# Reciprocal softmax sums stored in rows, gates and attention outputs laid out by token block, queries and keys asked for ahead

## The chip, the cores and the metric

The kernel runs on one NeuronCore of a Trainium2 chip. The metric is the device time of one execution in microseconds; beside the timed runs there is one profiled execution, whose trace is read here.

## What is computed

Two layers of a decoder trunk over 2048 tokens of width 1024, all in float32. Layer 0 runs two groups of eight heads side by side behind one input projection: latent attention (MLA, query and key of width 96) and forgetting attention (FoX, width 64, with a cumulative log forget gate added to the scores). Both are causal. Layer 1 is sliding-window attention with 16 query heads and 2 key heads. In each layer the attention output is multiplied by a SiLU gate, projected, added to the scaled input and normalized:

```
p = softmax(sc)                                   # causal, per head
o = concat([_merge(o_mla), _merge(o_fox)])        # 2048 x 1024
y = (o * silu(gate)) @ w_out
x = layer_norm(ALPHA * x + y)
```

The change touches layer 0 only: its softmax sums, its gate, its attention output and its query and key loads.

## The kernel before

Every matrix product is split: an operand is the sum of a high and a low part, and a product takes two or three matmuls. The program has five phases.

**Phase 1** (`phase1`) projects layer 0's input in chunks of 512 tokens. `feature_tile` applies the SiLU to a tile of 128 gate features by 512 tokens and stores it to the DRAM tensor `g1`, laid out [feature, token] (lines 349 to 352).

**Phase 2** (`phase2`) is layer 0's attention. It walks over 16 heads (even `n`: MLA, odd `n`: FoX) and, in each, over four chunks `c` of 512 queries. The generator `produce(n, c)` makes the scores and exponentials of four query blocks of 128; `consume(n, c)`, one chunk later, transposes the exponentials and multiplies them by the values (P V). The two are interleaved by hand: at each turn the one that is less far along goes on, by the weights of `weights`. `produce` loads the chunk's queries into `q0` (MLA: also `q1`), of which there are two buffers each; `load_head` loads a head's keys (`ka`, `kb`), values (`vv`) and, for FoX, the forget sums (`cb`), two buffers each, and is called at a head's first chunk (line 515). The softmax isn't normalized here. Each query block's sum of exponentials goes to a column of `su`; after four blocks `produce` takes reciprocals and stores them to the DRAM tensor `rd`, [head, token]. The tile holds one query per partition, so neighbouring tokens lie in different partitions and the store is made of single four-byte elements:

```
nc.vector.reciprocal(out=rec[:], in_=su[:])
nc.sync.dma_start(out=rd[h if mla else 8 + h, tcs].rearrange("(j p) -> p j", p=128), in_=rec[:])
```

`finish` in `consume` stores a chunk's output for one head to `og1[c]`, [128, 8, 512] (line 591).

**Phase 3** (`phase3`) is layer 0's output projection, block by block of 128 tokens. `load_og(t)` loads the block's gates into `oh`, the reciprocals into `ol` (each head's row of 128 tokens is read by 64 partitions), and the attention output into `og`, which has one buffer; POOL multiplies `og` by the gate, VectorE by the reciprocals, ScalarE and VectorE split it into high and low (lines 794 to 802). `out_block` makes 48 matmuls per block, adds the residual and collects the statistics; the normalization of two blocks is done together, in part on POOL (lines 759 to 773). The first two blocks are prepared at the end of phase 2 by `prefetch`, in one load of 256 tokens: POOL multiplies gate by reciprocals, then each block by that product (lines 649 to 654).

**Phases 4 and 5** are layer 1. Its reciprocal sums (`factors`) are transposed on TensorE and stored as 16 rows of 128 (lines 1074 to 1078).

Nearly all transfers are issued from SyncE's queue (SP). The order of each engine's instructions is set before the run by the framework: it goes by the order in which they are written, but moves one ahead when, by its own estimate, its inputs and its buffer are there earlier. On each queue they then run strictly in that order, each waiting for its semaphores. `keep_in_program_order` pins an instruction behind the one written before it on its engine.

Of the kernel before, what the change touches and what calls it, by code (L numbers as in the profile page):

```python
# [17 lines left out]
T = 2048  # L18
# [21 lines left out]
def decoder_trunk(ctx, tc, x, x_t, w_lat, w_main, w_u, g_lat, b_f, w_out1, ln1,  # L40
# [17 lines left out]
    kf = [dram.tile([8, 64, T], F32, name=f"kf{i}") for i in range(2)]  # L58
    vd = [dram.tile([2, 128, NB, 512], F32, name=f"vd{i}") for i in range(2)]
    cd = dram.tile([8, T], F32, name="cd")  # L60
    rd = dram.tile([16, T], F32, name="rd")
    g1 = dram.tile([D, T], F32, name="g1")
    og1 = [dram.tile([128, KB, 512], F32, name=f"og1_{c}") for c in range(4)]
    x1 = dram.tile([T, D], F32, name="x1")
    qs = [[dram.tile([16, 32, T], F32, name=f"qs{i}{s}") for s in range(2)] for i in range(2)]
    ks = [[dram.tile([2, 32, T], F32, name=f"ks{i}{s}") for s in range(2)] for i in range(2)]
# [119 lines left out]
    def phase1(late):  # L186
# [145 lines left out]
        def feature_tile(n, m, chunk, xT, w):  # L332

            (xh, xl), (wh, wl) = xT, w
            ms = tok(m)
            tcs = slice(chunk * 512, (chunk + 1) * 512)
            ps = ps_m.tile([128, 512], F32, name="pm")
            mm3(ps[:], [(wh[:, k, ms], wl[:, k, ms], xh[:, k, :], xl[:, k, :]) for k in range(KB)])
            if n < 4:
                dst = qf if n < 2 else kf  # L340
                p = (n % 2) * 2 + m
                hi = stg.tile([128, 512], F32R, name="s_hi")
                lo = stg.tile([128, 512], F32R, name="s_lo")
                split_ps(hi[:], lo[:], ps[:])
                for i, t in enumerate((hi, lo)):
                    nc.sync.dma_start(out=dst[i][2 * p:2 * p + 2, :, tcs].rearrange("h d t -> (h d) t"), in_=bits(t[:]))
            else:
                p = (n - 6) * 2 + m
                sg = stg.tile([128, 512], F32, name="s_x", bufs=3)
                nc.scalar.activation(out=sg[:], in_=ps[:], func=AF.Silu)  # L350
                queue = nc.gpsimd if (p, chunk) == (7, 3) else nc.sync
                queue.dma_start(out=g1[p * 128:(p + 1) * 128, tcs], in_=sg[:])

        k_heads = None
        sums = forget_sums(pool, fl, ps_t, ps_m)
# [118 lines left out]
            nc.sync.dma_start(out=cb[:], in_=cd[h:h + 1, :].broadcast_to([128, T]))  # L474
        return ka, kb_, vv, cb

    def load_gate(gt, rb, t0, n):

        nc.sync.dma_start(out=gt, in_=g1[:, t0:t0 + n].rearrange("(k p) t -> p k t", p=128))
        for s_ in range(2):  # L480
            nc.sync.dma_start(out=rb[s_ * 64:s_ * 64 + 64], in_=rd[:].rearrange("(k s) t -> s k t", s=2)[s_:s_ + 1, :, t0:t0 + n].broadcast_to([64, KB, n]))

    def phase2(ctx, kpool):
        pool = open_pool(ctx, "p2c", 1)
# [17 lines left out]
        def cuts(L):  # L502
# [3 lines left out]
                parts = [(0, 768), (768, 384)]  # L506
            return [(s0, w, 128 if w % 512 == 128 and w > 512 else 0) for s0, w in parts]

        def produce(n, c, st):

            mla = n % 2 == 0
            h = n // 2
            scale = MLA_SCALE if mla else DIM_SCALE
            if c == 0 and n not in heads:
                heads[n] = load_head(kpool, n)
            ka, kb_, vv, cb = heads[n]
            ds = slice(0, 96) if mla else slice(0, 128)
            tcs = slice(c * 512, (c + 1) * 512)
            q0 = qpool.tile([128, 512], F32R, name="q0")
            if mla:  # L520
                q1 = qpool.tile([128, 512], F32R, name="q1")
                for i, q in enumerate((q0, q1)):
                    nc.sync.dma_start(out=bits(q[0:64, :]), in_=qn[i][h, :, tcs])
                    for s_ in range(2):
                        nc.sync.dma_start(out=bits(q[64 + s_ * 16:80 + s_ * 16, :]), in_=qr[i][s_][h, :, tcs])
            else:
                nc.sync.dma_start(out=bits(q0[0:64, :]), in_=qf[0][h, :, tcs])
                nc.sync.dma_start(out=bits(q0[64:128, :]), in_=qf[1][h, :, tcs])
            su = sm.tile([128, 4], F32, name="su")
            rec = sm.tile([128, 4], F32, name="rec")  # L530
            for j in range(4):
                i = c * 4 + j
                L = (i + 1) * 128
                js = slice(j * 128, (j + 1) * 128)
                p = ppool.tile([128, T], F32, name="p")
                acc = None
                for s0, w, b in cuts(L):
                    last = s0 + w == L
                    S = ps_s.tile([128, 1024], F32, name="S")
                    for o in range(b - b % 512, b + w, 512):  # L540
# [12 lines left out]
                    if mla:  # L553
                        in1 = zm[:, 1152 - w:1152] if last else zm[:, 0:w]
                    else:
                        in1 = cb[:, s0:s0 + w]
                    a = sm.tile([128, 1], F32, name="mx")
                    nc.vector.tensor_tensor_reduce(out=p[:, s0:s0 + w], in0=S[:, b:b + w], in1=in1, op0=OP.add, op1=OP.min,  # L558
                                                   scale=-scale, scalar=3e38 if acc is None else acc[:], accum_out=a[:])
                    acc = a  # L560
                nc.scalar.activation(out=p[:, 0:L], in_=p[:, 0:L], func=AF.Exp, scale=-1.0, bias=acc[:], accum_out=su[:, j:j + 1])  # L561
                st.append(p)
                yield (i + 1) * (3 if mla else 2)
            nc.vector.reciprocal(out=rec[:], in_=su[:])
            nc.sync.dma_start(out=rd[h if mla else 8 + h, tcs].rearrange("(j p) -> p j", p=128), in_=rec[:])

        def consume(n, c, P):

# [17 lines left out]
            def finish(po):  # L586
                t2 = qpool.tile([64, 512], F32, name="t2")
                nc.scalar.copy(out=t2[:], in_=po[64:128, :])
                nc.vector.tensor_tensor(out=t2[:], in0=po[0:64, :], in1=t2[:], op=OP.add)  # L589
                queue = nc.gpsimd if (n, c) == (15, 3) else nc.sync  # L590
                queue.dma_start(out=og1[c][(hd % 2) * 64:(hd % 2) * 64 + 64, hd // 2, :], in_=t2[:])

            for g in range(c + 1):
                th = tpool.tile([128, 4, 512], F32R, name="th")
                tl = tpool.tile([128, 4, 512], F32R, name="tl")
                if g == c:
                    nc.gpsimd.memset(bits(th[:, 3, 256:384]), 0.0)
                    nc.gpsimd.memset(bits(tl[:, 3, 256:384]), 0.0)
                for j in range(4):
                    nk = j + 1 if g == c else 4  # L600
                    pt = ps_t.tile([128, 4, 128], F32, name="pt")
                    for k in range(nk):
# [29 lines left out]
        def wo_split(k, tag, raw, act=False):  # L632
# [2 lines left out]
            split_sb(v[:, 0:D], v[:, D:T], raw, act)  # L635
            wout[k] = (v[:, 0:D], v[:, D:T])

        def prefetch():

            raw = {}  # L640
# [4 lines left out]
            wout["raw"] = wo_load(kpool.tile([128, T], F32, name="cb"), 1, 0)  # L645
            ogs = kpool.tile([128, T], F32, name="cb")
            wout["og"] = [ogs[:, t * D:(t + 1) * D].rearrange("p (k q) -> p k q", q=128) for t in range(2)]
            gts, rbs = (ppool.tile([128, T], F32, name="p")[:].rearrange("p (k q) -> p k q", k=KB) for _ in range(2))
            load_gate(gts, rbs, 0, 256)
            for t in range(2):  # L650
                nc.sync.dma_start(out=wout["og"][t], in_=og1[0][:, :, tok(t)])
            nc.gpsimd.tensor_tensor(out=gts, in0=gts, in1=rbs, op=OP.mult)
            for t in range(2):
                nc.gpsimd.tensor_tensor(out=wout["og"][t], in0=wout["og"][t], in1=gts[:, :, tok(t)], op=OP.mult)
            for steps, k, tag in ((PRE[0], 7, "vv"), (PRE[1], 4, "ka"), (PRE[2], 6, "kb")):
                for _ in range(steps):
                    yield 1
                wo_split(k, tag, raw[k], True)
            for _ in range(99):
                yield 1  # L660
            wo_split(2, "vv", raw[2], True)
# [5 lines left out]
        for n, c in todo + [(None, None)]:  # L667
            st = []
            gens = []
            if (n, c) == (15, 3):  # L670
                r3, r5 = wo_load(kpool.tile([128, T], F32, name="cb"), 3, 5)
            if n is None:
                pre = prefetch()
                next(pre)
# [103 lines left out]
    def phase3(stack4, kpool, wout):  # L778
        with ExitStack() as ctx:
# [14 lines left out]
            def load_og(t):  # L794
                hl = parts()
                gt, rb = (bits(v[:]) for v in hl)
                load_gate(gt, rb, t * 128, 128)
                og = opool.tile([128, KB, 128], F32, name="og", bufs=1)
                nc.sync.dma_start(out=og[:], in_=og1[t // 4][:, :, tok(t % 4)])
                nc.gpsimd.tensor_tensor(out=og[:], in0=og[:], in1=gt, op=OP.mult)  # L800
                nc.vector.tensor_tensor(out=og[:], in0=og[:], in1=rb, op=OP.mult)
                return split_og(og[:], hl)
# [459 lines left out]
```

## Time and profile before

| | us |
|---|---|
| median of 3 runs | 2666.21 (2665.19 to 2668.59) |
| profiled execution | 2674.29 |
| span of the profiled execution, first to last instruction | 2672.5 |
| TensorE busy in it | 2471.1 (92%) |
| VectorE, ScalarE, POOL busy in it | 1531.1, 1172.7, 707.0 |

The span is what the rows count from: the times in them are microseconds from its start. A wait is put down to the instruction or transfer that ended it. TensorE's clock is granted at one of two levels; the profile gives it as a share of the full one. The share of the DMA engines is the time that the packets begun in a stretch took, so it can exceed 1.

### The profile page before, as it was taken

The page shows a single profiled execution, that of the slowest core. Times are in us where ns is not written, and L with a number is a line of the kernel's source. Part 1 is how long each engine was busy: PE and PEld are TensorE (multiplying, and loading weights), DVE is VectorE, ACT ScalarE, POOL GpSimd, SP SyncE. Part 2 cuts the span into 40 slices and gives each one's busy share as a digit, 9 for nine tenths or more (in the row PEclk, how much of TensorE's full clock was granted, in tenths as well). Part 3 has the DMA queues.
Part 4 walks back from the last instruction along what each step waited for, and adds up shares of the span by engine and source line. Part 5 has one row for each costly group of instructions (what it writes and reads, how often), then busy time and mean ns, then how long its engine had stood idle before and what let it go on. Part 6 is the DMA issues. An engine that isn't in the chain of part 4 may idle for free.

```text
span 2672.5 us, 36349 instructions
## 1 busy us (share of the span) xinstructions
PE 2471.1 (92%) x12885; PEld 2050.3 (77%) x12885; DVE 1531.1 (57%) x3002; ACT 1172.7 (44%) x2409; POOL 707.0 (26%) x694
## 2 busy tenths in 40 slices
PE   8999999999999999999999787659999999999997
PEld 7898888987788887888877665437888887777775
DVE  5442264317787877777777643345633644777775
ACT  3121222217676866777676501011121115566663
POOL 2010011101222221222222333232321321356555
PEclk9999999999999999999999888879999999999998
DMA  6574346654556665454554558854444653566563
GB/s 204 177 251 143 106 152 235 202 167 62 95 93 93 83 114 86 83 111 79 97 84 83 115 151 170 151 129 156 142 138 141 177 154 100 150 150 165 155 155 103
DMA packets 298566, 360.91 MB, mean 135 GB/s; under 512 B 55920, under 2 KB 202352, under 8 KB 293776
## 3 DMA queue, kind: packets, MB, share of 16 engines
q1 hardware_dynamic: 294224, 343.51, 53.6%
q0 software_dynamic: 4160, 15.08, 1.5%
q8 instruction: 102, 1.67, 0.3%
q14 instruction: 80, 0.66, 0.2%
HBM read 240.20 MB, written 118.29 MB: 134 GB/s over the span
## 4 chain that ended last, share of the span: by engine, by line
PE 68%; DMA 17%; DVE 5%; POOL 3%; ACT 3%; issue 3%; SPq 1%; POOLq 0%; DVEq 0%; ACTq 0%
PE pm L91 11%; PE pm L89 11%; PE pm L90 10%; PE pt L604 6%; DMA og<-og 5%; PE S L547 4%; PE S L548 4%; PE po L581 3%; PE po L582 3%; DMA kb<-kf 3%; DMA q<-qr 3%; DMA q<-qf 2%; PE S L1061 2%; PE py L727 2%; PE S L550 2%
## 5 line engine op out<-in xcount | busy, mean ns | idle before, releaser
L76 DVE TENSOR_TENSOR tl<-pt,th 128x512 fp32r<-128x512 f32 (+3 forms) x672 | 400.7, 611 | 128.4 <-ACT th L75 125.2
L89 PE MATMUL pm<-xh,w 128*128 128x512 f32 x1088 | 428.7, 394 | 7.5 <-DVE z L734 5.6
L75 ACT CAST th<-pt 128x512 fp32r<-128x512 f32 (+3 forms) x672 | 340.4, 524 | 203.2 <-PE pt L604 168.1
L91 PE MATMUL pm<-xh,w 128*128 128x512 f32 x1088 | 425.9, 392 | 0.0
L90 PE MATMUL pm<-xl,w 128*128 128x512 f32 x1088 | 425.6, 391 | 0.0
L604 PE MATMUL pt<-ident,p 128*128 128x128 f32 x2176 | 348.0, 280 | 4.0 <-DVE tl L76 3.9
L561 ACT ACTIVATE p<-p,mx 128x128 f32<-128x128 f32 (+15 forms) x256 | 309.0, 1207 | 29.3 <-DVE mx L558 27.5
L604 PEld LDWEIGHTS pt<-ident,p 128*128 128x128 f32 x2176 | 271.8, 145 | 58.6 <-DVE tl L76 7.3
L547 PE MATMUL S<-ka,q 96*128 96x512 f32 (+5 forms) x640 | 253.4, 396 | 29.6 <-DMA q<-qf 11.5
L581 PE MATMUL po<-th,vv 128*128 128x512 f32 (+2 forms) x640 | 278.0, 434 | 0.6 <-DVE t L589 0.4
L82 POOL TENSOR_SCALAR w<-w_raw 128x1024 fp32r<-128x1024 f32 (+3 forms) x88 | 98.5, 1132 | 581.3 <-PE pm L91 418.8
L89 PEld LDWEIGHTS pm<-xh,w 128*128 128x128 f32 x1088 | 205.0, 188 | 49.5 <-issue 7.3
L582 PE MATMUL po<-tl,vv 128*128 128x512 f32 (+2 forms) x640 | 238.3, 373 | 0.0
L91 PEld LDWEIGHTS pm<-xh,w 128*128 128x128 f32 x1088 | 204.7, 188 | 42.9
L90 PEld LDWEIGHTS pm<-xl,w 128*128 128x128 f32 x1088 | 204.9, 188 | 41.6
L609 POOL TENSOR_SCALAR th<-tf 128x512 fp32r<-128x512 f32 x96 | 59.4, 618 | 668.8 <-ACT tf L608 363.8
L548 PE MATMUL S<-kb,q 96*128 96x512 f32 (+5 forms) x640 | 234.4, 369 | 0.0
L83 DVE TENSOR_TENSOR w<-w_raw,w 128x1024 fp32r<-128x1024 f32 (+3 forms) x89 | 138.6, 1572 | 130.4 <-POOL w L82 127.4
L558 DVE CUSTOM_DVE_ANT_0 p<-S,zm 128x1024 f32<-128x1024 f32 (+7 forms) x128 | 123.7, 967 | 104.4 <-PE S L550 103.4
L547 PEld LDWEIGHTS S<-ka,q 128*128 128x128 f32 (+1 forms) x640 | 124.5, 194 | 54.5 <-issue 23.3
L1062 DVE CUSTOM_DVE_ANT_0 p<-S,bm,nsk 128x256 f32<-128x256 f32 x256 | 117.7, 477 | 71.8 <-PE S L1061 69.7
L1064 ACT ACTIVATE p<-p,mx 128x256 f32<-128x256 f32 x256 | 129.0, 505 | 66.2 <-DVE mx L1062 65.7
(249 smaller groups left out, 4771.0 us busy)
## 6 DMA issues: line engine op xcount, KB each, us to landing
w_raw<-in_w_main_dram SPq DMA_DIRECT2D x40, 512.0 KB, 5.2
w_raw<-in_w_odd_dram SPq DMA_DIRECT2D x36, 512.0 KB, 4.5
vd<-s_v SPq DMA_DIRECT2D x64, 256.0 KB, 2.7
vv<-vd SPq DMA_DIRECT2D x16, 1024.0 KB, 10.6
qs<-hl SPq DMA_DIRECT2D x64, 256.0 KB, 3.5
qt<-qs SPq DMA_DIRECT2D x64, 256.0 KB, 5.3
ka<-kf SPq DMA_DIRECT2D x16, 512.0 KB, 9.4
kb<-kf SPq DMA_DIRECT2D x16, 512.0 KB, 9.0
```

The costliest lines, as they stand in the source:

```text
L75: nc.scalar.copy(out=hi, in_=src)
L76: nc.vector.tensor_tensor(out=lo, in0=src, in1=bits(hi), op=OP.subtract)
L83: nc.vector.tensor_tensor(out=lo, in0=src, in1=bits(hi), op=OP.subtract)
L89: nc.tensor.matmul(ps, lhsT=ah, rhs=bh, start=(i == 0), stop=False)
L90: nc.tensor.matmul(ps, lhsT=ah, rhs=bl, start=False, stop=False)
L91: nc.tensor.matmul(ps, lhsT=al, rhs=bh, start=False, stop=(i == n - 1))
L547: nc.tensor.matmul(dst, lhsT=q0[ds, js], rhs=ka[ds, ks_], start=True, stop=False)
L548: nc.tensor.matmul(dst, lhsT=q0[ds, js], rhs=kb_[ds, ks_], start=False, stop=not (mla or diag))
L561: nc.scalar.activation(out=p[:, 0:L], in_=p[:, 0:L], func=AF.Exp, scale=-1.0, bias=acc[:], accum_out=su[:, j:j + 1])
L581: nc.tensor.matmul(po[0][:, q_:512], lhsT=vv[:, kb, :], rhs=th[:, k, q_:512], start=(kb == 0), stop=False)
L582: nc.tensor.matmul(po[0][:, q_:512], lhsT=vv[:, kb, :], rhs=tl[:, k, q_:512], start=False, stop=(kb == c * 4 + 3))
L604: nc.tensor.transpose(out=pt[:, k, :], in_=P[j][:, kk:kk + 128], identity=ident[:])
```

## The change

`g1` becomes [block, partition, 8, 128], `og1[c]` becomes [4 blocks, partition, 8, 128] and `rd` becomes [block, 2, 8, 128], so that what one block of 128 tokens needs is contiguous: 4 KB per partition of gates and of outputs, and for each half of the partitions one row of 4 KB of reciprocals. The stores to `g1` and `og1` are split accordingly, into four runs of 512 B per partition. The reciprocals of a head are kept in a tile of 16 columns; `store_sums`, called from `consume`, transposes it on TensorE and stores 16 rows of 512 B: once per head, and for the last head once per chunk. `load_q` asks for the queries of the next chunk at the start of each; the keys and values of head `n + 1` are asked for in chunk 1 of head `n`. The gates and reciprocals of block 0 are loaded in the last chunk of the last head into tiles of their own; those of block 1 by `prefetch`; VectorE instead of POOL multiplies the two blocks by gate and reciprocals, after the three weight splits.

```diff
-    rd = dram.tile([16, T], F32, name="rd")
-    g1 = dram.tile([D, T], F32, name="g1")
-    og1 = [dram.tile([128, KB, 512], F32, name=f"og1_{c}") for c in range(4)]
+    rd = dram.tile([NB, 2, KB, 128], F32, name="rd")
+    g1 = dram.tile([NB, 128, KB, 128], F32, name="g1")
+    og1 = [dram.tile([4, 128, KB, 128], F32, name=f"og1_{c}") for c in range(4)]
...
-                queue.dma_start(out=g1[p * 128:(p + 1) * 128, tcs], in_=sg[:])
+                queue.dma_start(out=g1[chunk * 4:chunk * 4 + 4, :, p, :].rearrange("j p t -> p j t"), in_=sg[:].rearrange("p (j t) -> p j t", j=4))
...
+    def load_gate(gt, rb, t):
+
+        nc.sync.dma_start(out=gt, in_=g1[t])
         for s_ in range(2):
+            nc.sync.dma_start(out=rb[s_ * 64:s_ * 64 + 64], in_=rd[t, s_:s_ + 1].broadcast_to([64, KB, 128]))
...
+            if (n, c) not in queries:
+                queries[n, c] = load_q(n, c)
+            q0, q1 = queries.pop((n, c))
+            after = (n, c + 1) if c < 3 else (n + 1, 0)
+            if after[0] < 16:
+                queries[after] = load_q(*after)
+            if c == 1 and n + 1 < 16:
+                heads[n + 1] = load_head(kpool, n + 1)
             su = sm.tile([128, 4], F32, name="su")
-            rec = sm.tile([128, 4], F32, name="rec")
+            if c == 0:
+                recs[n] = sm.tile([128, 16], F32, name="rec", bufs=3)
...
-            nc.vector.reciprocal(out=rec[:], in_=su[:])
-            nc.sync.dma_start(out=rd[h if mla else 8 + h, tcs].rearrange("(j p) -> p j", p=128), in_=rec[:])
+            nc.vector.reciprocal(out=recs[n][:, c * 4:c * 4 + 4], in_=su[:])
+
+        def store_sums(n, b0, b1):
+
+            hd = n // 2 + 8 * (n % 2)
+            pt = ps_t.tile([128, 4, 128], F32, name="pt")
+            nc.tensor.transpose(out=pt[0:b1 - b0, 0, :], in_=recs[n][:, b0:b1], identity=ident[:])
+            rt = sm.tile([16, 128], F32, name="rt", bufs=1)
+            nc.scalar.copy(out=rt[0:b1 - b0, :], in_=pt[0:b1 - b0, 0, :])
+            nc.sync.dma_start(out=rd[b0:b1, hd % 2, hd // 2, :], in_=rt[0:b1 - b0, :])
...
+                    if j == 2 and g == min(c, 2):
+                        if n == 15:
+                            store_sums(n, c * 4, c * 4 + 4)
+                        elif c == 3:
+                            store_sums(n, 0, NB)
...
-            load_gate(gts, rbs, 0, 256)
+            gates = [early, [v.rearrange("p (k q) -> p k q", q=128) for v in halves(ppool.tile([128, T], F32, name="p")[:])]]
+            load_gate(*gates[1], 1)
...
-            nc.gpsimd.tensor_tensor(out=gts, in0=gts, in1=rbs, op=OP.mult)
-            for t in range(2):
-                nc.gpsimd.tensor_tensor(out=wout["og"][t], in0=wout["og"][t], in1=gts[:, :, tok(t)], op=OP.mult)
...
+            for t in range(2):
+                for v in gates[t]:
+                    tc.keep_in_program_order(nc.vector.tensor_tensor(out=wout["og"][t], in0=wout["og"][t], in1=v, op=OP.mult))
...
             if (n, c) == (15, 3):
                 r3, r5 = wo_load(kpool.tile([128, T], F32, name="cb"), 3, 5)
+                early = [pool.tile([128, KB, 128], F32, name=f"early{i}")[:] for i in range(2)]
+                load_gate(*early, 0)
...
-                load_gate(gt, rb, t * 128, 128)
+                load_gate(gt, rb, t)
                 og = opool.tile([128, KB, 128], F32, name="og", bufs=1)
-                nc.sync.dma_start(out=og[:], in_=og1[t // 4][:, :, tok(t % 4)])
+                nc.sync.dma_start(out=og[:], in_=og1[t // 4][t % 4])
```

## Rows read from the trace of the kernel before

**Rows 1.** Windows: length; busy of PE, PEld, DVE, ACT, POOL; PEclk, DMA share, GB/s.

```profile
594.00:1500.00 906.00, 862.01 (x5107) 723.17 (x5106) 682.39 (x1426) 650.22 (x1201) 200.21 (x315) 0.97 0.54 89
1500.00:1560.00 60.00, 39.76 (x184) 32.36 (x183) 24.89 (x30) 15.13 (x25) 19.18 (x15) 0.80 0.64 137
1560.00:1850.00 290.00, 197.24 (x751) 152.41 (x750) 126.18 (x145) 38.28 (x40) 96.48 (x75) 0.84 0.68 152
1850.00:2264.00 414.00, 413.17 (x1901) 339.83 (x1900) 190.15 (x243) 93.90 (x181) 100.20 (x78) 1.00 0.47 144
```

**Rows 2.** Waits of PE, 594 to 1500: us in total, times, longest.

```profile
PE S L550 <- DMA q<-qr: 13.0, 7, 2.9
PE S L547 <- DMA q<-qf: 11.5, 6, 2.7
PE S L547 <- DMA q<-qr: 7.9, 3, 3.9
```

**Rows 3.** Chain of waits, 988 to 1010: start, us, what.

```profile
995.97 10.56 DMA q<-qf
```

**Rows 4.** Timeline of SP, 978 to 1004: start, us, engine, line, transfer.

```profile
983.80 0.38 SPq L565 DMA_DIRECT2D rd<-rec  x1
...
985.27 0.58 SPq L465 DMA_DIRECT2D kb<-kp  x1
...
994.96 0.38 SPq L565 DMA_DIRECT2D rd<-rec  x1
```

**Rows 5.** Windows of 2 us, columns as in rows 1.

```profile
982.00:984.00 2.00, 2.00 (x16) 1.74 (x15) 0.64 (x4) 2.00 (x4) 0.00 (x0) 1.00 0.88 231
...
986.00:988.00 2.00, 2.00 (x16) 1.65 (x14) 0.96 (x3) 1.50 (x3) 1.46 (x2) 1.00 0.00 0
...
1006.00:1008.00 2.00, 1.33 (x4) 1.17 (x5) 0.00 (x0) 0.00 (x0) 0.00 (x0) 0.62 0.23 73
```

**Rows 6.** DMA issues, whole span: count, KB each, median us to landing.

```profile
q<-qf SPq DMA_DIRECT2D x64, 128.0 KB, 4.4
z<-in_x_dram SPq DMA_DIRECT2D x16, 512.0 KB, 5.3
...
gt<-g SPq DMA_DIRECT2D x16, 512.0 KB, 4.9
...
rd<-rec SPq DMA_DIRECT2D x64, 2.0 KB, 11.3
...
rs<-rt SPq DMA_DIRECT2D x16, 8.0 KB, 1.4
```

**Rows 7.** Line 1075, layer 1's transpose of sums: ns min/median/max, first, last start.

```profile
L1075 PE MATMUL pt<-ident,rc x16: 270/271/416, 2257.1 to 2633.5; 128*16 128x128 f32 x16
```

**Rows 8.** Chain of waits, 1694 to 1760.

```profile
1696.37 2.34 POOL og L800
...
1712.22 2.42 POOL og L800
...
1718.39 18.17 DMA og<-og
...
1736.69 2.34 POOL og L800
```

**Rows 9.** Line 800, POOL's multiplication by the gate, whole span.

```profile
L800 POOL TENSOR_TENSOR og<-og,oh x14: 2327/2356/2407, 1562.3 to 1817.8; 128x1024 f32<-128x1024 f32 x14
```

**Rows 10.** A window of 2 us in the output projection, columns as in rows 1.

```profile
1684.00:1686.00 2.00, 2.00 (x11) 1.65 (x10) 0.00 (x0) 0.00 (x0) 0.00 (x0) 1.00 0.89 45
```

**Rows 11.** Line 799, the 14 loads of `og`: time from issue to landing.

```profile
DMA to landing us min/median/max: 10.5/14.6/18.7
```

**Rows 12.** Waits of PE, 1500 to 1850.

```profile
PE py L727 <- POOL oh L82: 17.1, 1, 17.1
```

**Rows 13.** Chain of waits, 1505 to 1545.

```profile
1503.45 25.32 DMA p<-rd
```

**Rows 14.** Waits of SP, 594 to 1500, at the load of values.

```profile
SPq L470 <- PE pt L604: 64.4, 14, 6.6
```

More of the change, by code (lines that the diff above doesn't have):

```diff
@@ L475, in load_head @@
         return ka, kb_, vv, cb
-    def load_gate(gt, rb, t0, n):
-        nc.sync.dma_start(out=gt, in_=g1[:, t0:t0 + n].rearrange("(k p) t -> p k t", p=128))
+    def load_gate(gt, rb, t):
+        nc.sync.dma_start(out=gt, in_=g1[t])
         for s_ in range(2):
-            nc.sync.dma_start(out=rb[s_ * 64:s_ * 64 + 64], in_=rd[:].rearrange("(k s) t -> s k t", s=2)[s_:s_ + 1, :, t0:t0 + n].broadcast_to([64, KB, n]))
+            nc.sync.dma_start(out=rb[s_ * 64:s_ * 64 + 64], in_=rd[t, s_:s_ + 1].broadcast_to([64, KB, 128]))
     def phase2(ctx, kpool):
@@ L507, in cuts, with load_q @@
             return [(s0, w, 128 if w % 512 == 128 and w > 512 else 0) for s0, w in parts]
+        queries = {}
+        def load_q(n, c):
+            h = n // 2
+            tcs = slice(c * 512, (c + 1) * 512)
+            q0 = qpool.tile([128, 512], F32R, name="q0")
+            if n % 2:
+                for i in range(2):
+                    nc.sync.dma_start(out=bits(q0[i * 64:i * 64 + 64, :]), in_=qf[i][h, :, tcs])
+                return q0, None
+            q1 = qpool.tile([128, 512], F32R, name="q1")
+            for i, q in enumerate((q0, q1)):
+                nc.sync.dma_start(out=bits(q[0:64, :]), in_=qn[i][h, :, tcs])
+                for s_ in range(2):
+                    nc.sync.dma_start(out=bits(q[64 + s_ * 16:80 + s_ * 16, :]), in_=qr[i][s_][h, :, tcs])
+            return q0, q1
         def produce(n, c, st):
@@ L518, in produce @@
             tcs = slice(c * 512, (c + 1) * 512)
[L519 to L528, printed above, removed]
+            if (n, c) not in queries:
[6 more added lines that the diff above has]
+                heads[n + 1] = load_head(kpool, n + 1)
             su = sm.tile([128, 4], F32, name="su")
-            rec = sm.tile([128, 4], F32, name="rec")
+            if c == 0:
+                recs[n] = sm.tile([128, 16], F32, name="rec", bufs=3)
             for j in range(4):
@@ L563, in produce @@
                 yield (i + 1) * (3 if mla else 2)
-            nc.vector.reciprocal(out=rec[:], in_=su[:])
-            nc.sync.dma_start(out=rd[h if mla else 8 + h, tcs].rearrange("(j p) -> p j", p=128), in_=rec[:])
+            nc.vector.reciprocal(out=recs[n][:, c * 4:c * 4 + 4], in_=su[:])
+        recs = {}
+        def store_sums(n, b0, b1):
[5 more added lines that the diff above has]
+            nc.sync.dma_start(out=rd[b0:b1, hd % 2, hd // 2, :], in_=rt[0:b1 - b0, :])
         def consume(n, c, P):
@@ L590, in finish @@
                 queue = nc.gpsimd if (n, c) == (15, 3) else nc.sync
-                queue.dma_start(out=og1[c][(hd % 2) * 64:(hd % 2) * 64 + 64, hd // 2, :], in_=t2[:])
+                queue.dma_start(out=og1[c][:, (hd % 2) * 64:(hd % 2) * 64 + 64, hd // 2, :].rearrange("j p t -> p j t"), in_=t2[:].rearrange("p (j t) -> p j t", j=4))
             for g in range(c + 1):
@@ L636, in wo_split, with halves @@
             wout[k] = (v[:, 0:D], v[:, D:T])
+        def halves(t):
+            return t[:, 0:D], t[:, D:T]
         def prefetch():
@@ L647, in prefetch @@
             wout["og"] = [ogs[:, t * D:(t + 1) * D].rearrange("p (k q) -> p k q", q=128) for t in range(2)]
-            gts, rbs = (ppool.tile([128, T], F32, name="p")[:].rearrange("p (k q) -> p k q", k=KB) for _ in range(2))
-            load_gate(gts, rbs, 0, 256)
+            gates = [early, [v.rearrange("p (k q) -> p k q", q=128) for v in halves(ppool.tile([128, T], F32, name="p")[:])]]
+            load_gate(*gates[1], 1)
             for t in range(2):
-                nc.sync.dma_start(out=wout["og"][t], in_=og1[0][:, :, tok(t)])
-            nc.gpsimd.tensor_tensor(out=gts, in0=gts, in1=rbs, op=OP.mult)
-            for t in range(2):
-                nc.gpsimd.tensor_tensor(out=wout["og"][t], in0=wout["og"][t], in1=gts[:, :, tok(t)], op=OP.mult)
+                nc.sync.dma_start(out=wout["og"][t], in_=og1[0][t])
             for steps, k, tag in ((PRE[0], 7, "vv"), (PRE[1], 4, "ka"), (PRE[2], 6, "kb")):
```

## The prediction

> **What bounds the kernel now.** I read the page first: TensorE is busy 92% of the span and heads the chain of waits, so only time in which TensorE stands still, or runs at a low granted clock, can be won. I then cut the span into stages. The reader is to see in [rows 1] that the projections of layer 1 (1850 to 2264 us) leave TensorE no gap at clock 1.00, while layer 0's attention (594 to 1500) leaves it idle for 906.0 - 862.0 = 44 us at clock 0.97, the crossing into the output projection (1500 to 1560) for 20 us at 0.80, and layer 0's output projection (1560 to 1850) for 93 us at 0.84. The changed lines work in these last three.
>
> In the attention the list of waits, taken for that stage alone, gives the cause: the first score product of a chunk waits for its query load, 13.0 + 11.5 + 7.9 = 32.4 us in 16 waits of at most 3.9 us [rows 2]. One of them, followed back in the chain: the load was issued at 995.97 and took 10.56 us to land [rows 3]; the median of that load is 4.4 us [rows 6]. SyncE's queue shows what stood ahead of it: a store of reciprocal sums at 983.80, the last key load of the next head at 985.27, and another store of sums at 994.96 [rows 4]. Windows of 2 us show what the transfers did: 231 GB/s just before the first store of sums, and 0 GB/s from 986 to 988 with that key load still under way [rows 5]. The store moves 2 KB and needs 11.3 us; the same sort of sums, stored as rows in layer 1 (8 KB), needs 1.4 us [rows 6]. I read this as: 512 separate four-byte writes hold up what is queued behind them for most of those 11 us, four times per head. The clock falls after such a wait (0.62 from 1006 to 1008 [rows 5]).
>
> In the output projection the chain goes once per block through the load of the attention output, POOL's multiplication by the gate, VectorE's by the reciprocals, ScalarE's and VectorE's split, and back to the load, because the tile `og` has one buffer. From the multiplication at 1712.22 to the next issue at 1718.39 are 6.2 us; the load then takes 18.17 us [rows 8]. Two blocks take 1736.69 - 1696.37 = 40.3 us: the even half, 15.85 us, is bound by POOL, which does the normalization of two blocks in between; the odd half by the transfer. TensorE needs far less: 413.17 us / 1901 = 0.217 us per instruction at full clock [rows 1], so 48 x 0.22 = 10.6 us per block, 21 per pair. At 1684 to 1686 the transfers are busy (share 0.89) and move only 45 GB/s [rows 10]: `z`, gates and reciprocals were issued ahead of `og`, and what is being read then is the reciprocals, in runs of 512 B, each by 64 partitions.
>
> **The change part by part.**
>
> *Sums.* 64 stores of four-byte elements go; 19 stores of rows come (15 heads once, the last head four times). Each costs a transpose of the form that layer 1 has, 0.271 us on TensorE [rows 7]: 19 x 0.27 = 5.1 us, all on the path, since TensorE is the bound there. The copy out is ScalarE's, which is busy 650 of 906 us [rows 1]; without that cover TensorE would wait for a transpose buffer. The 64 reciprocals stay. What the removal gives lies between 0 (if the key loads are slow by themselves) and all 32.4 us of waits plus the clock, 906 x 0.03 = 27 us. A query load that lands in 4.4 instead of 10.56 us comes 6 us sooner, which is more than the longest wait, 3.9. So I stand near the upper end: 29 of the waits, 23 of the clock, less 5: **47 us** (bounds -5 and 54). Late next: nothing on the load side; TensorE itself.
>
> *Queries and keys asked for ahead.* I cost this at nothing. The number of buffers is unchanged, and in the old kernel the query and key loads already stand in SyncE's queue as far ahead as their buffers come free: the chunk that waited at 1006 had its load issued one chunk earlier [rows 3]. Writing the request earlier changes a rank in the order, not a buffer. The last head's early gate load (three DMAs) joins SyncE's queue in the last chunk; it lies beside that chunk's score products.
>
> *Gates and outputs by block.* Per block the gates and `og` become runs of 4 KB per partition, and the reciprocals one 4 KB row read by 64 partitions. Run length by itself gives little: a quiet 512 KB load of 512 B runs lands in 4.9 us (`gt`), one of 4 KB rows in 5.3 (`z` from `in_x`) [rows 6]. What can fall is the stretch at 45 GB/s. Bounds for the load of `og` afterwards: 4.9 us, as layer 1's, and 10.5, the shortest landing of the 14 in this stage [rows 11]; I take 6, near the lower end, as the reciprocals become an eighth as many reads. A pair then takes 15.85 + 6.2 + 6 = 28.1 us, still over TensorE's 21. From the first to the last of the 14 multiplications are 1817.8 - 1562.3 = 255.5 us [rows 9], 13 steps or 6.5 pairs: 6.5 x 28.1 = 183, so **73 us** go (at 10.5: 255.5 - 6.5 x 32.6 = 44; at best, if POOL's normalization also leaves the chain, 6.5 x 23 = 150, so 106).
>
> *The stores by block.* 32 gate stores and 64 output stores go from 2 KB runs to 512 B runs. Their extra cost lies between 0 and the difference of the quiet landings above, about half a microsecond each. I take nothing, since only the staging tiles wait for them (three in the projections, two in the attention) and TensorE's work of the next tiles lies over them; without that cover it is 96 x 0.5 = 48 us. The Trainium skill, Perfetto Trace Analysis, DMA Optimizations, speaks against this part: it says that transfers under 2 KB carry much overhead each and should be merged, and here they are cut. By it the stores would be dearer and the sum smaller by up to those 48 us; the quiet landings [rows 6] do not show such a difference for loads, and no row shows it for stores of 512 B runs over 128 partitions.
>
> *The crossing.* TensorE waited 17.1 us for the first block [rows 12], behind the load of the reciprocals of two blocks, 25.32 us [rows 13], which stood behind the last store of sums. Now block 0's gates come one chunk earlier, that store is short, and the products of gate and output move from POOL to VectorE (four, each at most the 2.36 us of POOL's form [rows 9]), beside the last P V products. I leave 2 us of the wait: **15 us** (bounds 0 and 17). The load of `og` for the third block, the first that is not made ahead, is in the chain too; from the median, 14.6 us [rows 11], to 6 are **9 us** more (bounds 0 and 9).
>
> Sum: 47 + 73 + 15 + 9 = 144 us (bounds of all four together: 39 and 186). The profiled execution took 2674.29 us (span 2672.5), so it would take 2530; the median of the runs, 2666.21, is 8 us lower, so **2522 us**.
>
> **The rivals.**
> *The attention's waits stay.* The key loads come as 8 KB rows to half the partitions in the same stretch; if these, not the sums, hold up the queries, the attention gains nothing and pays 5: 2666 - 97 + 5 = 2574. Against it: the same key loads ran at 231 GB/s before the store of sums [rows 5]. 14 in 100.
> *The output projection stays slow.* If 64 partitions reading one row are slow at any run length, or the order of SyncE's queue still puts three loads ahead of `og`, the load stays at 10.5 us and the crossing with it: 47 + 44 = 91, so 2575. Against it: the reads of that row become an eighth as many. The Trainium skill, DMA: Bandwidth & Descriptors, Specifications, puts line rate at runs of 512 B and more, by which the new layout brings nothing here; the quiet landings agree, the 45 GB/s does not. 14 in 100.
> *Better still.* POOL's order shifts with the earlier loads, and normalization leaves the chain: 54 + 106 + 17 + 9 = 186, so 2480. 6 in 100.
> *Slower: SyncE stands at a value load.* The next head's values are now asked for in chunk 1, but their buffer comes free only when the last P V product of the head before is done, in chunk 2. SyncE already stands there 14 times, 64.4 us in all, at most 6.6 [rows 14]. If it stood there for a whole chunk, the queries of chunk 3 would queue behind it. It outweighs the gain from 144 / 15 = 9.6 us per head on; at 12 us per head the time is 2522 + 180 = 2702. 4 in 100.
> *Nothing comes of it*, because the framework's order undoes each part: 2666. 2 in 100.
>
> **How the numbers follow.** The forecast has 60 in 100, its own range 2490 to 2560. With the better case and the two half cases 94 in 100 are faster. The range 2470 to 2600 holds forecast, better case and half cases with the edges of their costs, and leaves out the last two and some of the tails. A change of 0.2%, 5 us, is about what can be told from none: faster 0.94, same 0.02, slower 0.04.
>
> **What would show it.** Attention: no query wait over 1 us, clock 0.99, the stage 40 to 55 us shorter, rows of sums landing in under 3 us. Output projection: `og` landing in 5 to 8 us, pairs of 26 to 31 us, clock above 0.84. Crossing: first block within 3 us of the last P V product. I am wrong if the query load still takes 10 us with no store of sums ahead of it, if the stretch at 45 GB/s is still there, or if VectorE's four products hold up the last P V.

## The result, and the profile after

The changed kernel takes **2521.57 us** (median of 4 runs, 2520.3 to 2524.9), the kernel before beside it 2667.4 (4 runs, 2665.19 to 2673.32): a ratio of 0.9452, 95% interval 0.9434 to 0.947. The profiled execution took 2524.90 us, its span 2523.1, the mean granted clock 0.984 of full speed.

Three stretches of the changed kernel, with the columns of [rows 1]: layer 0's attention, its output projection with the crossing into it, and the projections of layer 1.

```profile
598.00:1462.60 864.60, 854.64 (x5207) 720.48 (x5205) 696.77 (x1448) 666.22 (x1241) 206.53 (x323) 0.99 0.38 98
...
1460.00:1690.00 230.00, 192.51 (x797) 151.68 (x796) 131.90 (x149) 40.27 (x42) 97.81 (x76) 0.92 0.62 201
1690.00:2104.00 414.00, 412.51 (x1897) 339.67 (x1895) 192.23 (x241) 86.80 (x162) 103.42 (x81) 1.00 0.46 143
```

The attention has 10.0 us without TensorE work left and runs at 0.99; the output projection is up from 0.84 to 0.92 and its transfers from 152 to 201 GB/s; layer 1's projections are as they were. The stages are best cut where TensorE goes from one to the next. These are the lines that show it, the products of P V, the weight loads of the output projection and its last product, for the kernel before and then for the changed one (in the first two of each fence duration in ns, first and last start in us; in the third start and duration in us):

```profile
L582 PE MATMUL po<-tl,vv x640: 278/393/629, 619.8 to 1521.9; 128*128 128x512 f32 x160
...
L727 PEld LDWEIGHTS py<-ka,oh x64: 186/188/334, 1539.2 to 1832.1; 128*128 128x128 f32 x64
...
1835.48 0.40 PE L729 MATMUL py<-wo_hi,ol 128*128 128x512 f32 x1
```

```profile
L609 PE MATMUL po<-tl,vv x640: 276/393/628, 621.6 to 1462.5; 128*128 128x512 f32 x160
...
L764 PEld LDWEIGHTS py<-ka,oh x64: 186/188/330, 1463.8 to 1689.4; 128*128 128x128 f32 x64
...
1692.80 0.40 PE L766 MATMUL py<-wo_hi,ol 128*128 128x512 f32 x1
```

The first score product starts at 598.0 and 598.7, and layer 0's last output product at 1835.5 and 1692.8. So the attention, from the first score product to the last P V product, went from 923.9 to 863.8 us (60 less), the crossing, from there to the first weight load of the projection, from 17.3 to 1.3 (16 less), the output projection from 296.3 to 229.0 (67 less). From there to the end of the span it is 837.0 and 830.3 us (7 less; 5.6 of them a wait of TensorE for VectorE's `z`, just behind that point in the kernel before, which is gone). The four make 150; less the 0.7 of the later start this is the 149.4 by which the spans differ.

The list of TensorE's waits over the attention, which answers to [rows 2] (us in total, times, longest):

```profile
PE S L567 <- DMA q<-qr: 2.9, 1, 2.9
PE S L564 <- DVE mx L575: 2.4, 9, 0.5
PE pt L636 <- DVE tl L76: 2.3, 1, 2.3
```

The sixteen waits for queries are one, at the first head. The transfers, median us to landing (last figure), beside [rows 6]:

```profile
q<-qf SPq DMA_DIRECT2D x64, 128.0 KB, 3.3
q<-qr SPq DMA_DIRECT2D x128, 32.0 KB, 2.4
og<-og SPq DMA_DIRECT2D x14, 512.0 KB, 3.9
ol<-rd SPq DMA_DIRECT2D x28, 256.0 KB, 8.1
rd<-rt SPq DMA_DIRECT2D x15, 8.0 KB, 2.1
```

A store of sums lands in 2.1 us instead of 11.3, and the load of `og` in 3.9 instead of 14.6 [rows 11]. One pair of blocks in the chain of waits of the output projection, beside [rows 8] (start, us, what):

```profile
1574.87 2.40 POOL og L837
...
1584.08 2.42 POOL z L808
1586.56 3.25 POOL z L809
...
1590.76 2.42 POOL og L837
...
1596.92 7.04 DMA og<-og
1604.12 2.39 POOL og L837
```

The even half (1574.87 to 1590.76, 15.9 us) is still POOL with the normalization of two blocks; the odd half is 6.2 us of splitting and 7.0 of load. A pair is 29.3 us instead of 40.3.

### The profile page after: what moved, and what is told of

Same layout as the page of the kernel before. It is cut to its first block, busy times and chain, and to the rows that moved or that the text cites. A ratio compares the mean times of both kernels' runs of the same rounds, so it can differ in the third digit from the quotient of the medians.

```text
span 2523.1 us, 36278 instructions
## 1 busy us (share of the span) xinstructions
PE 2430.5 (96%) x12904; PEld 2024.0 (80%) x12904; DVE 1533.4 (61%) x3006; ACT 1176.2 (47%) x2428; POOL 698.3 (28%) x691
## 3 DMA queue, kind: packets, MB, share of 16 engines
q1 hardware_dynamic: 244032, 343.51, 47.2%
## 4 chain that ended last, share of the span: by engine, by line
PE 83%; DVE 5%; POOL 4%; DMA 3%; ACT 3%; issue 2%; SPq 0%; DVEq 0%; POOLq 0%; ACTq 0%
PE pm L89 11%; PE pm L91 11%; PE pm L90 11%; PE pt L636 9%; PE po L608 5%; PE S L564 5%; PE po L609 5%; PE S L565 5%; PE S L567 3%; PE S L1098 2%; PE py L764 2%; PE py L766 2%; PE py L765 2%; PE pt L1127 2%; DMA og<-og 2%
## 5 line engine op out<-in xcount | busy, mean ns | idle before, releaser
L636 PE MATMUL pt<-ident,p 128*128 128x128 f32 x2176 | 341.5, 274 | 2.6 <-DVE tl L76 2.3
L636 PEld LDWEIGHTS pt<-ident,p 128*128 128x128 f32 x2176 | 265.2, 141 | 56.6 <-issue 5.4
L764 PE MATMUL py<-wo_hi,oh 128*128 128x512 f32 x320 | 129.9, 406 | 11.8 <-DVE ve L784 9.5
```

What stands on the lines that cost most here:

```text
L636: nc.tensor.transpose(out=pt[:, k, :], in_=P[j][:, kk:kk + 128], identity=ident[:])
L764: nc.tensor.matmul(ps[:], lhsT=oh(k), rhs=wh[:, ms], start=(n == 0), stop=False)
```

## The experiments

Two theories stood against each other for each stage. For the attention: the stores of single four-byte elements hold up the query loads, against: the loads were late, and asking ahead cured it. For the output projection: the reads of the reciprocals in runs of 512 B by 64 partitions were slow, against: the gates and outputs in short runs were, or the order of POOL's work. The kernel before took 2638 to 2643 us on the two chips of these runs (2667 above), so each ratio is to the kernel before that ran beside it on the same chip.

| run | median us | ratio, 95% interval | last P V product starts at |
|---|---|---|---|
| e1_sums | 2593.64 | 0.9813, 0.9795 to 0.9832 | 1453.5 |
| e2_layout | 2865.29 | 1.0829, 1.0778 to 1.0881 | 1802.9 |
| e3_ahead | 2644.68 | 0.9999, 0.9986 to 1.0012 | 1497.7 |
| e4_no_ahead | 2520.93 | 0.9535, 0.9516 to 0.9554 | 1460.7 |
| e5_four_bytes | 2577.43 | 0.9751, 0.9732 to 0.9769 | 1516.8 |
| e6_sixteen_bytes | 2521.48 | 0.954, 0.9525 to 0.9555 | |
| e7_rd_old | 2580.61 | 0.9763, 0.9747 to 0.9779 | |
| e8_gates_old | 2527.42 | 0.9565, 0.955 to 0.9581 | |
| e9_product | 2516.3 | 0.9541, 0.9522 to 0.956 | |
| e10_product_start | 2525.01 | 0.9569, 0.9551 to 0.9587 | |
| e11_start | 2525.62 | 0.9571, 0.9556 to 0.9586 | |
| e12_four_bytes_apart | 2876.44 | 1.0884, 1.0814 to 1.0953 | 1809.3 |

**e1_sums.** The kernel before with the sums of a head transposed and stored in rows, into the old `rd`.

```diff
-            nc.sync.dma_start(out=rd[h if mla else 8 + h, tcs].rearrange("(j p) -> p j", p=128), in_=rec[:])
+            nc.sync.dma_start(out=rd[hd].rearrange("(b p) -> b p", p=128)[b0:b1, :], in_=rt[0:b1 - b0, :])
```

> The kernel before with one part of the change: the sums are transposed and stored in rows, the tensor rd keeps its layout [head, token]. Theory (the four-byte stores hold up the query loads): the attention stage loses the 55 to 60 us that it lost in the whole change, the output projection stays, so about 2667 - 60 = 2607. Rival (the key loads as 8 KB rows hold them up, or it is the asking ahead that helps): no less than 2660, since only the transposes come in.

It takes 49.6 us less than the kernel before on the same chip (2643.27), clear of the noise, though less than the 55 to 60 expected. With the query loads written where they were, TensorE waits for a query 0.3 us in all:

```profile
PE S L548 <- DMA q<-qn: 0.3, 1, 0.3
```

The crossing, too, is 9.2 us in this run, where e3_ahead, with the old stores and the old layout, has 17.0.

**e3_ahead and e4_no_ahead.** The kernel before with the requests for queries, keys and values ahead and nothing else; the changed kernel without them.

```diff
-            if (n, c) not in queries:
-                queries[n, c] = load_q(n, c)
...
-            if after[0] < 16:
-                queries[after] = load_q(*after)
-            if c == 1 and n + 1 < 16:
-                heads[n + 1] = load_head(kpool, n + 1)
```

> The kernel before with one part: queries asked for one chunk ahead, keys and values in chunk 1 of the head before. Theory: nothing, 2667 within 6. Rival (late requests cause the waits): the 32 us of query waits and their clock go, 2600 to 2625.

> The changed kernel without the asking ahead (query and head loads written as in the kernel before). Theory: 2522 within 6. Rival (asking ahead does part of it): 2535 or more, with query waits back in the attention.

Asking ahead is worth nothing by either. In e3_ahead the list of TensorE's waits over the attention still shows what [rows 2] shows:

```profile
PE S L566 <- DMA q<-qr: 10.1, 5, 2.9
PE S L563 <- DMA q<-qr: 7.1, 4, 2.6
PE S L563 <- DMA q<-qf: 5.7, 4, 2.5
```

e4_no_ahead is also 72.7 us below e1_sums on the same chip: that is the layout by block together with the early gate load and the move of two blocks' products to VectorE, all with the sums in rows.

**e2_layout.** The kernel before with the three layouts by block alone; the four-byte stores go into the new `rd`.

```diff
-            nc.sync.dma_start(out=rd[h if mla else 8 + h, tcs].rearrange("(j p) -> p j", p=128), in_=rec[:])
+            nc.sync.dma_start(out=rd[c * 4:c * 4 + 4, hd % 2, hd // 2, :].rearrange("j p -> p j"), in_=rec[:])
```

> The kernel before with one part: gates, outputs and reciprocals by block of 128 tokens; the sums are still stored as four-byte elements, nothing is asked for ahead. Theory: the output projection loses about 65 us and the crossing into it a few, the attention stage nothing: about 2595. Rival (the projection got faster because the last store of sums and the early gate load left its start): a gain under 20 us, 2647 or more.

The expectation was missed: the run is 222 us slower than the kernel before. The output projection did get short (from its first weight load at 1810.4 to the next transposes at 2038.7 it is 228 us, in e3_ahead, on the same chip and with the old layout, 1514.7 to 1807.9, 293), but the attention ends 305 us later than in e3_ahead. The list of TensorE's waits from 594 to 1750:

```profile
PE S L550 <- DMA q<-qr: 76.9, 17, 13.9
PE S L547 <- DMA q<-qf: 59.7, 7, 12.7
PE po L582 <- DVE t L590: 29.3, 4, 9.5
```

The expectation took the price of a four-byte store to be one and the same wherever it goes. What the layout changes for it is the address: four pieces of 512 B, each 8 KB from the next, in place of one piece of 2 KB.

**e5_four_bytes, e6_sixteen_bytes, e12_four_bytes_apart.** The changed kernel with one store more after each reciprocal, of the same 2 KB to a tensor that nothing reads: in 512 elements of 4 bytes; in 128 runs of 16; in 512 elements of 4, with e2_layout's addresses.

```diff
+            nc.sync.dma_start(out=rx[n, tcs].rearrange("(j p) -> p j", p=128), in_=recs[n][:, c * 4:c * 4 + 4])   # e5
+            nc.sync.dma_start(out=rx[n, tcs].rearrange("(p j) -> p j", j=4), in_=recs[n][:, c * 4:c * 4 + 4])   # e6
+            nc.sync.dma_start(out=rx[c * 4:c * 4 + 4, n % 2, n // 2, :].rearrange("j p -> p j"), in_=recs[n][:, c * 4:c * 4 + 4])   # e12
```

> The changed kernel with the old form of store added back as an extra: after each chunk the reciprocals also go to a DRAM tensor that nobody reads, 512 elements of four bytes, 64 times. Theory: the attention's waits come back, 45 to 65 us, the output projection stays: 2567 to 2587. Rival (the sums were not what held up the queries, or the new order of requests now covers it): under 2535.

> The same extra store of 2 KB, 64 times, but as 128 runs of 16 bytes. If the number of separate writes is what holds up the queue, a quarter of them hold it up for a quarter of the time, 2 to 3 us, less than the query loads now have to spare: 2522 to 2532. If any write far under 512 bytes does it, however many: near the run with 512 elements, 2560 or more.

> The changed kernel with one more store after each reciprocal, 512 elements of 4 bytes as in e5_four_bytes, but into four pieces of 512 bytes that lie 8 KB apart (the address pattern of e2_layout) in place of one piece of 2 KB. Theory: it is the address pattern of these stores that made e2_layout slow, and neither the number of elements (equal in both) nor something else of the old kernel. Then the attention gets longer by 200 to 300 us, as in e2_layout, and the time is 2720 to 2820 us. Rival: 64 stores of 512 elements cost the same wherever they go, and e2_layout was slow through something else, such as its query loads standing behind the stores of og in short runs: then the time is that of e5_four_bytes, 2570 to 2590 us.

e6 takes what the changed kernel takes; e5, on the same chip, 56 us more (0.9 per store); e12 355 more than the changed kernel (5.5 per store; above the range named). So 2 KB in 128 runs of 16 bytes cost nothing that shows here and in 512 elements of 4 bytes they do (whether by the size or the number of the elements, these runs do not separate), and the addresses multiply the price by six. That is what made e2_layout slow, whose number of elements was the old one. The layout of `rd` by block is only to be had together with the stores in rows. In e5 TensorE waits 29.3 us for queries again, and the landings (median us, last figure) of what shares the queue are late again:

```profile
rx<-rec SPq DMA_DIRECT2D x64, 2.0 KB, 10.2
kb<-kf SPq DMA_DIRECT2D x16, 512.0 KB, 15.2
q<-qr SPq DMA_DIRECT2D x128, 32.0 KB, 6.6
rd<-rt SPq DMA_DIRECT2D x15, 8.0 KB, 13.0
```

where e6's extra store lands in 1.8. In e12, SyncE's timeline (start, us) and windows of 2 us (columns as above) behind one extra store:

```profile
1006.38 0.38 SPq L583 DMA_DIRECT2D rx<-rec  x1
1012.15 0.56 SPq L471 DMA_DIRECT2D vv<-vd  x1
1013.80 7.00 SPq L620 DMA_DIRECT2D og<-t  x1
```

```profile
1008.00:1010.00 2.00, 2.00 (x16) 1.81 (x15) 1.54 (x4) 1.40 (x4) 0.00 (x0) 1.00 0.00 0
1010.00:1012.00 2.00, 2.00 (x15) 1.67 (x14) 1.79 (x5) 1.91 (x3) 1.34 (x2) 1.00 0.00 0
...
1018.00:1020.00 2.00, 2.00 (x15) 1.72 (x15) 1.73 (x5) 1.98 (x4) 0.00 (x0) 1.00 1.35 21
1020.00:1022.00 2.00, 2.00 (x13) 1.65 (x12) 2.00 (x5) 1.45 (x3) 0.81 (x2) 1.00 0.56 4
```

Nothing moves for some 4 us, longer than the 2 us of [rows 5]. Then the transfers behind it move 35, 103 and 19 GB/s in the three windows left out, and 21 and 4 in the two shown, and SyncE needs 7.00 us to issue one store of attention outputs. That is no single case: the longest issue of this store in a run is 8.8 us in the kernel before, 7.6 in e5 and 10.7 in e12, all with four-byte stores, and 1.1 in the changed kernel and 0.9 in e6; the median is 0.5 to 0.6 in each. So what is queued behind four-byte stores is late twice, in its issue and in its transfer.

**e7_rd_old and e8_gates_old.** The changed kernel with the old `rd` (rows stored as in e1_sums); with the old `g1` and `og1`.

```diff
-            nc.sync.dma_start(out=rb[s_ * 64:s_ * 64 + 64], in_=rd[t, s_:s_ + 1].broadcast_to([64, KB, 128]))
+            nc.sync.dma_start(out=rb[s_ * 64:s_ * 64 + 64], in_=rd[:].rearrange("(k s) t -> s k t", s=2)[s_:s_ + 1, :, t * 128:t * 128 + 128].broadcast_to([64, KB, 128]))
...
-        nc.sync.dma_start(out=gt, in_=g1[t])
+        nc.sync.dma_start(out=gt, in_=g1[:, t * 128:t * 128 + 128].rearrange("(k p) t -> p k t", p=128))
...
-                nc.sync.dma_start(out=og[:], in_=og1[t // 4][t % 4])
+                nc.sync.dma_start(out=og[:], in_=og1[t // 4][:, :, tok(t % 4)])
```

> The changed kernel with the reciprocals kept as [head, token], so that a block's reciprocals are read in runs of 512 B again, each by 64 partitions; gates and outputs stay by block. Theory (these reads are what is slow): most of the output projection's 67 us come back, 2575 to 2590, with stretches at about 45 GB/s. Rival (the gates and outputs in 4 KB runs matter): under 2540.

> The opposite: gates and outputs in the old layouts, runs of 512 B, and reciprocals by block in one row of 4 KB. Theory: close to the changed kernel, 2522 to 2535, the load of og a little slower than 3.9 us. Rival: 2560 or more.

Against e6 on the same chip, the reads of the reciprocals are worth 59 us, the gates and outputs 6. In e7 the load of `og` lands in 9.0 us, and the busy stretch without throughput of [rows 10] is back; the first window below is of e7, the second of the changed kernel, also during a load of `og`:

```profile
1598.00:1600.00 2.00, 2.00 (x11) 1.65 (x10) 0.00 (x0) 0.00 (x0) 0.00 (x0) 1.00 0.99 47
```

```profile
1602.00:1604.00 2.00, 2.00 (x11) 1.61 (x10) 0.00 (x0) 0.00 (x0) 0.00 (x0) 1.00 1.00 393
```

The DMA share is 0.99 and 1.00, the throughput 47 and 393 GB/s. Over the whole output projection, windows of 2 us with a share over 0.8 and less than 100 GB/s number 17 in the kernel before (from 1540 to 1836), 5 in e7, and none in the changed kernel and in e8.

**e9_product, e11_start, e10_product_start.** Two tries at what is left in the output projection: POOL multiplies gate by reciprocals before `og` has come, and VectorE alone touches `og` (e9; `z` has four buffers instead of five, for space); layer 1's first transposes are released at block 15 instead of 12 (e11); both (e10).

```diff
-                nc.gpsimd.tensor_tensor(out=og[:], in0=og[:], in1=gt, op=OP.mult)
-                nc.vector.tensor_tensor(out=og[:], in0=og[:], in1=rb, op=OP.mult)
+                gp = opool.tile([128, KB, 128], F32, name="gp", bufs=1)
+                nc.gpsimd.tensor_tensor(out=gp[:], in0=gt, in1=rb, op=OP.mult)
+                nc.vector.tensor_tensor(out=og[:], in0=og[:], in1=gp[:], op=OP.mult)
...
-                if t == 12:
+                if t == 15:
```

> A try at what is late next in the output projection: POOL multiplies gate by reciprocals into a tile of its own (one z buffer less for the room), and only VectorE touches og, so POOL's 2.4 us leave the way from the load of og to TensorE. If the chain of one block sets the time, it gets shorter by 2.4 us per block, 13 x 2.4 = 31, at most down to TensorE's own pace: 2490 to 2505. If POOL's order (product, normalization of two blocks, product) sets it, the pairs stay near 29 us: 2515 to 2525.

> The changed kernel with layer 1's first transposes and weight load written after block 15 instead of block 12. In the changed kernel TensorE stands 14.6 us at these transposes in the middle of block 13. If that wait is on the path, up to 10 us go: 2511 to 2520. If the chain through og sets the end of the stage anyway, or the transposes now stand at its end: 2520 to 2530.

> Both edits together. If both waits are on the path their gains add up: 2480 to 2495. If POOL's order sets the pace: as the better of the two.

e9 has the lowest time, 5 us (0.2%) below the changed kernel's, but its ratio to the kernel before is no lower than that of e4, on another chip: a lead that isn't settled. Of the 9.7 us between the two profiled spans 5 lie ahead of the edited lines (the last P V product starts at 1457.4 instead of 1462.5). e10 and e11 are 3 to 4 us above the changed kernel; e10 was expected to be at least as good as the better of the two, and it isn't. The chain of e9's output projection says why e9 doesn't give more: `og` is out of this pair, and what comes last is the reciprocals.

```profile
1564.38 2.40 POOL gp L838
...
1576.84 3.26 POOL z L809
...
1581.06 2.36 POOL gp L838
...
1584.86 7.88 DMA ol<-rd
1592.91 2.40 POOL gp L838
```

A pair is 28.5 us. In e11 TensorE's wait for these transposes, 14.6 us in the changed kernel (below), is 10.4 in three waits behind the output projection, and the clock there is lower (0.74 from 1680 to 1700). The stage itself ends sooner: from the last multiplication to the last output product are 16.5 us (1662.4 to 1678.9) instead of 29.1. The wait was moved and not removed.

## Why the prediction was right, point by point

The forecast was 2522 us and the median is 2521.57. The mechanisms hold, but that the number is met within 1 us is luck. The attention gave 13 more than its term and the crossing 1, the output projection gave 15 less, and 7 came from behind it, where the forecast has nothing: 150 in place of 144. The median then lies 3.3 us below the profiled execution, where 8 were put in.

**Attention: forecast 47, measured 60.** The mechanism holds: e1_sums removes the waits with nothing asked ahead, e5 brings the same kind of waits back with nothing else changed. The term was mis-sized: 60 lies outside its own bounds (-5 and 54) and above the 40 to 55 that the forecast named as its sign. Time without TensorE work fell from 47.2 (876.83 us busy in the 924.0 from 598 to 1522) to 10.0 us, so by 37 where 29 was put in. The forecast took the waits that name a query load; the same list for the kernel before has two more, which also went:

```profile
PE S L547 <- issue: 3.5, 1, 3.5
PE S L547 <- DMA kb<-kf: 3.1, 1, 3.1
```

The busy time fell from 876.83 to 854.64, by 22, with 5 us of transposes added: so 27 that go with the higher clock, where 23 was put in. The condition "no query wait over 1 us" failed at one place, the first head (2.9), where no store of sums stands ahead. Beside the experiments' kernel before, sums alone gave 49.6, for attention and crossing together (the attention is 902.1 us in e3_ahead and 857.2 in e1_sums, 45 less), and e3_ahead, which keeps the four-byte stores, had 22.9 us of query waits where [rows 2] has 32.4: the size of this term is not the same in the two sets of runs.

**Asked ahead: forecast 0, measured 0** (e3, e4). The rival in which SyncE stands at the value load did not come: it waits there as often as in [rows 14] and half as long again,

```profile
SPq L470 <- PE pt L636: 99.8, 14, 7.5
```

99.8 us in place of 64.4, but never a chunk, and no query is late behind it. The forecast's other sign of being wrong, VectorE's four products holding up the last P V, hardly shows either: TensorE waits 0.6 us for VectorE there, once, at 1461.45.

**Crossing: forecast 15, measured 16.** The first block starts 1.3 us after the last P V product. Sums in rows alone leave 9.2 us of the crossing (e1) and the layout by block alone 7.5 (e2), against 17.0 in e3_ahead on that chip; the early gate load and VectorE's products were not tried by themselves.

**Output projection: forecast 73 + 9 = 82, measured 67.** Line 837, the 14 multiplications, beside [rows 9], and line 836, the loads of `og`, beside [rows 11]:

```profile
L837 POOL TENSOR_TENSOR og<-og,oh x14: 2350/2388/2410, 1477.7 to 1663.7; 128x1024 f32<-128x1024 f32 x14
```

```profile
DMA to landing us min/median/max: 3.5/3.9/8.3
```

From first to last they now take 186.0 us (forecast 183): 69.5 of the 73. The pair was put at 15.85 + 6.2 + 6 = 28.1 and is 15.9 + 6.2 + 7.0 with 0.2 between them; the median landing of 3.9 is below the forecast's window of 5 to 8, but in the pair shown the load that counts, that of the odd half, takes 7. (The 23 us per pair in the forecast's best case come without a working, and no run shows such a pair.) From the first product of the projection to the first multiplication it is 13.9 us instead of 23.1: the forecast 9. What the forecast missed is that its sum ended at the last multiplication. Behind it come 1692.8 - 1663.7 = 29.1 us where the kernel before has 17.7, so 11 were given back. The timelines of TensorE show the place, the kernel before first:

```profile
1800.58 1.11 PE L146 MATMUL pt<-ident,xh 128*128 128x128 f32 x4 [12.77 <-DVE xl L76]
```

```profile
1657.67 1.12 PE L146 MATMUL pt<-ident,xh 128*128 128x128 f32 x4 [14.61 <-DVE xl L76]
```

Layer 1's transposes stand in TensorE's order ahead of the last blocks' products, and their input is late. In the kernel before this wait ended 17 us ahead of the last multiplication at 1817.8 and TensorE then waited for `og` anyway; now it ends 6 us ahead of it, and the products of the last blocks queue up behind it. e11_start shows that it is this wait: without it 16.5 us come behind the last multiplication. It also shows that releasing the transposes later only carries the wait behind the stage.

**Which reads count.** The forecast put the weight on the reciprocals and little on run length, and e7 and e8 agree: 59 and 6 us. The Trainium skill, DMA: Bandwidth & Descriptors, Specifications, puts line rate at runs of 512 B and more. By that rule e7 should have cost nothing; it cost 59 us. For e8, whose gates and outputs are read once, in the same run length, the rule nearly holds. So it is not the run length alone that made the reciprocals slow; which part of the rest does (64 partitions reading one row, or rows 16 KB apart) no run separates.

**The stores by block: forecast 0.** The projections ahead of the attention (0 to 594 us) keep TensorE busy for 581.2 us with the cut stores and 581.5 without, and e8, which has the long stores back, is slower. The Trainium skill, Perfetto Trace Analysis, DMA Optimizations, warns of transfers under 2 KB. Each of these stores moves 128 or 256 KB, and only the runs in it are short; the forecast applied the warning to the runs. The price that it weighed, up to 48 us, does not show here. In the attention, e4 with its 861.7 us is longer than e1_sums on the same chip (857.2), but e8, with the long stores, has 861.4; 2.5 of the difference are the first head's query wait, 2.8 us in e4, 2.4 in e8 and 0.3 in e1_sums.

**The kernel before, twice.** The forecast's 2522 is made against 2666. Beside the experiments the kernel before took 2638 to 2643, on two chips that agree, and kernels like the changed one still 2521 (e4, e6). There the same change is worth some 122 us. e3_ahead, with the old stores, ends its attention at 1497.7 where the kernel before of the result ends it at 1521.9: 24 us earlier, so most of the difference lies there. That it is the four-byte stores whose price differs is likely, and not shown; whether the chip makes the difference is open, since the chip of the first result is not on record.

## What to carry to other kernels

The small store was priced here by its elements and where they go, and not by its 2 KB, and the price was paid by the loads queued behind it: look in the timeline of the queue for what stood ahead of a late load before moving the load forward. Transpose such a tile on TensorE and store rows before the layout of the target is spread out by block: the layout without the rows cost 222 us (e2). When a chain is shortened, ask at its end which wait was hidden under it, as the transposes were here.

## What was not expected of the hardware

- 512 elements of 4 bytes in one piece of 2 KB cost 0.9 us of the kernel per store, the same elements in four pieces 8 KB apart 5.5 us (e5, e12); 128 runs of 16 bytes nothing that can be told (e6).
- Behind such stores SyncE itself stood: the longest issue of an output store took 8.8 us in the kernel before and 10.7 in e12, 1.1 in the changed kernel.
- The kernel before took 24 to 29 us less beside the experiments than beside the first result, the changed one and its like (e4, e6) agree within 1.
